# First pair of half-size products with plain work inside it, and a scan insert that ends with the state, in a Mamba-2 layer on one core

## The chip, the cores and the metric

The kernel runs on one core of a Trainium2 chip. Its time is the device time of one execution in microseconds (us). The core's engines run side by side: PE (TensorE) does the matmuls, ACT (ScalarE), DVE (VectorE) and POOL (GpSimd) the elementwise work, SP (SyncE) issues most of the transfers. Weights are loaded into PE on a path of its own (PEld in the profile).

## The reference

One layer of a hybrid trunk, cut to what is computed here (batch 1, 512 tokens, width 2048, 64 heads of 64 in 8 groups, state 128, all in float32):

```python
hn = rmsnorm(x, ln_g)
proj = hn @ w_in                      # z, (x, B, C), dt
xbc = silu(causal_depthwise_conv(xbc, conv_w, conv_b))
dt = softplus(dt + dt_bias); a = -exp(a_log)
# per chunk, for every head:
y_diag = einsum("blsg,blsgr,bsgrp->blgrp", cb, decay, xc)
y_off  = einsum("blgn,bgrpn,blgr->blgrp", cc, state, exp(cs))
new_state = state * exp(last) + einsum("bsgn,bsgr,bsgrp->bgrpn", bc, w_in, xc)
y = y_diag + y_off + d_skip * xs
y = rmsnorm(y * silu(z), norm_g)
out = rmsnorm(x + y @ w_out, final_g)
```

The in-projection has 80 column tiles of 128 (32 of z, 32 of x, 8 of B and 8 of C), the out-projection goes from 4096 to 2048.

## The kernel before

**Numbers in two parts.** Every float32 matmul is done in three, on a rounded part `hi` and a rest `lo`. `split_piece` (L84 to L89) makes both for a piece of weights: ACT casts `hi` (L87), DVE subtracts to get `lo` (L88). PE cannot use a piece before DVE is done with its `lo`.

**In-projection.** The first eight column tiles (B0, C0, x0, z0, x1, z1, B1, C1) are done plainly: `mm_k` (L198) runs 16 k-steps of six matmuls, 256 wide each. The other 72 tiles are done in 36 pairs by a scheme with seven half-size products instead of eight (`pair`, L639; each `product`, L635 to L637, has 24 matmuls of 256). The weights of the products are the quarters R11, R22, R21 and sums of quarters T1, T2, T3, T4: `q_fetch` adds a quarter in by an accumulating transfer of POOL, `q_add` (L604) adds on DVE. The product T4 of a pair is not run at once but handed to the next pair as `prev`, and runs there between the second and the third product: in a steady pair PE's order is R11, T1, the T4 of the pair before, T2, R22, R21, T3. The first pair has no such `prev`: its order is T1, R11, (nothing for four steps), R22, T2, R21, T3. R11 and T1 write the banks `S` and `R`, and so do T2 and R22 after them.

**Steps and events.** A step is the work of PE between two calls of `run`: one k-step of six matmuls of 256, or three of 512, about 0.68 us. A pair has 28. Whatever is to be done beside the matmuls is an event at a step (`add`, L704), and `run(step)` issues the events of a step just before its matmuls. PE, SP and POOL execute in the order of the code; on DVE and ACT a scheduler of the framework orders the instructions. `q_events` sets when the loads, sums and splits of a pair are issued, relative to the pair's first step `b`; `x_form3` (L571 to L578, steps 114 to 126) rewrites half of the activations `xh` and `xl` in place for the third product, over a temporary `xr` that the tiles' own normalization (L398) uses too.

**The scan.** Each of the 32 units (two heads) has six events: load, decay (12 exps on ACT, L456 to L459, and a product `m` on DVE, L461), transposes of x (L473, with `xd` and `xw` on DVE), state (four matmul records, L488, then split into `stsh` on ACT and `stsl` on DVE, L403 and L404), yd (16 records, L502 and L506, then DVE's D-skip, L509) and yo (L518 to L520, then DVE, L521 to L523). State and yd of a unit are due in the same step, b+9 of a pair; g_bt (L416) makes the transpose of B for a group and g_cb (L433 to L436) its products.

**Out-projection.** Plain pieces (`mm_o`, L929 to L931: 512 wide, six matmuls for each of four token tiles t) and two chains of four half-size pairs (`opair`, L867 to L869) alternate: 12 plain pieces, chain 1, eight plain pieces, chain 2, then plain pieces to the end. The chains use sums of quarters of y as well (`y_fetch` L822, `y_forms` L841 to L848, f11, f1, f2 and so on, each split into h and l). In a chain the first pair has no `prev` and the same order T1, R11, nothing, R22, T2 as above. L889 subtracts the T1 product from `acc`, L902 the R22 product and L907 the T2 product, L912 adds R21's; T3's is copied on ACT (L916). `get_out` loads and splits the plain pieces; every fourth goes to buffers of its own.

The list that follows shows the functions the diff touches and their callers.

## Time and profile before

| | us |
|---|---|
| median of 3 runs | 1294.51 (1292.67 to 1301.33) |
| profiled execution, its own time | 1295.7 |
| its span, first to last instruction | 1294.0 |
| mean granted clock of PE | 0.991 of full speed |
| PE, DVE, ACT busy | 1252.1, 1084.3, 826.6 |
| ACT's casts of whole pieces, all / DVE's splits of whole pieces, mean each | 1.05 / 1.22 |

The share of the span by engine in the profile's first part says which engine bounds the whole, the waits of PE say at which places another one does. Where a wait is named by a line, that line is where the awaited result was made.

### The profile page before, as it was taken

Reading aid. Unit: us, or ns where it says so; the run is one execution under the profiler, and the core shown is the slowest. Engines: PE = TensorE matmul, PEld = TensorE weight load, DVE = VectorE, ACT = ScalarE, POOL = GpSimd, SP = SyncE. Lnnn points to the kernel's source line nnn. Section 1 sums busy time; section 2 is a strip of 40 time slices with the busy share of each in tenths; the row PEclk is TensorE's granted clock in tenths of the full one; section 3 lists DMA queues with packets and bytes.
Section 4 is the critical chain, followed back from the end, with each engine's and each line's share of the span. In section 5 each row is a group of like instructions: output and inputs, shape, how many; then the busy total and the mean of one; then the engine's idle time right before and its main releaser. Section 6 shows DMA issues by size and latency. Waiting matters only on the chain.

```text
span 1294.0 us, 24519 instructions
## 1 busy us (share of the span) xinstructions
PE 1252.1 (97%) x9932; PEld 1192.9 (92%) x9932; DVE 1084.3 (84%) x1449; ACT 826.6 (64%) x1357; POOL 77.5 (6%) x99
## 2 busy tenths in 40 slices
PE   8989899999999999999999999999999899999997
PEld 8989899999999999999999999999988899899885
DVE  5796988988989898998889899889857877887865
ACT  7667667677666757767685867778666445434433
POOL 0000001010000101010100001000000000000000
PEclk9989999999999999999999999999999999999999
DMA  9546657585676667667667677766637576647612
GB/s 356 179 141 172 162 161 174 143 215 142 192 197 174 159 169 183 164 176 199 162 161 195 151 188 171 212 155 154 185 105 258 146 199 199 197 119 229 183 57 98
DMA packets 70194, 225.90 MB, mean 175 GB/s; under 512 B 8384, under 2 KB 12800, under 8 KB 69952
## 3 DMA queue, kind: packets, MB, share of 16 engines
q1 hardware_dynamic: 56688, 176.34, 40.2%
q0 software_dynamic: 12672, 46.14, 22.1%
q8 instruction: 78, 1.28, 0.4%
q10 hardware_dynamic: 720, 1.84, 0.4%
q14 instruction: 36, 0.29, 0.1%
HBM read 211.52 MB, written 12.78 MB: 173 GB/s over the span
## 4 chain that ended last, share of the span: by engine, by line
PE 74%; DVE 11%; DMA 7%; issue 4%; ACT 3%; SPq 0%; POOL 0%; DVEq 0%; ACTq 0%; POOLq 0%
PE S L637 7%; PE S L635 7%; PE S L636 7%; PE mm L635 5%; PE mm L636 4%; PE R L635 4%; PE mm L637 4%; PE R L636 4%; PE R L637 4%; DVE lo L88 3%; PE mm L929 3%; PE mm L931 3%; PE mm L930 3%; PE yd L502 2%; PE mm L867 2%
## 5 line engine op out<-in xcount | busy, mean ns | idle before, releaser
L87 ACT CAST hi<-ra 128x1024 fp32r<-128x1024 f32 x150 | 154.7, 1046 | 159.5 <-DVE ra L604 72.9
L88 DVE TENSOR_TENSOR lo<-ra,hi 128x1024 fp32r<-128x1024 f32 x150 | 181.3, 1221 | 24.2 <-ACT hi L87 24.1
L635 PE MATMUL mm<-xh,hi 128*128 128x256 f32 x576 | 163.6, 284 | 0.0
L637 PE MATMUL mm<-xh,lo 128*128 128x256 f32 x576 | 160.6, 279 | 0.6 <-DVE lo L88 0.6
L636 PE MATMUL mm<-xl,hi 128*128 128x256 f32 x576 | 160.4, 278 | 0.0
L637 PE MATMUL R<-s,lo 128*128 128x256 f32 x576 | 160.3, 278 | 0.1
L635 PE MATMUL R<-s,hi 128*128 128x256 f32 x576 | 160.2, 278 | 0.0
L636 PE MATMUL R<-s,hi 128*128 128x256 f32 x576 | 160.2, 278 | 0.0
L88 DVE TENSOR_TENSOR lo<-rc,hi 128x1024 fp32r<-128x1024 f32 x94 | 114.9, 1223 | 28.5 <-ACT hi L87 28.1
L87 ACT CAST hi<-rc 128x1024 fp32r<-128x1024 f32 x94 | 98.4, 1047 | 50.8 <-issue 29.1
L604 DVE TENSOR_TENSOR ra<-ra,rc 128x1024 f32<-128x1024 f32 x88 | 107.7, 1224 | 13.3 <-DMA rc<-in_wi 11.8
L635 PEld LDWEIGHTS mm<-xh,hi 128*128 128x128 f32 x576 | 108.1, 188 | 5.2 <-issue 5.0
L637 PEld LDWEIGHTS mm<-xh,lo 128*128 128x128 f32 x576 | 109.2, 190 | 0.8 <-DVE lo L88 0.8
L637 PEld LDWEIGHTS R<-s,lo 128*128 128x128 f32 x576 | 109.1, 189 | 0.3 <-DVE lo L88 0.3
L635 PEld LDWEIGHTS R<-s,hi 128*128 128x128 f32 x576 | 108.2, 188 | 0.0
L636 PEld LDWEIGHTS mm<-xl,hi 128*128 128x128 f32 x576 | 108.2, 188 | 0.0
L636 PEld LDWEIGHTS R<-s,hi 128*128 128x128 f32 x576 | 108.1, 188 | 0.0
L637 PE MATMUL S<-xh,lo 128*128 128x256 f32 x288 | 83.5, 290 | 5.6 <-DVE lo L88 5.6
L635 PE MATMUL S<-xh,h1h 128*128 128x256 f32 x288 | 83.4, 290 | 1.0 <-DVE xr L398 1.0
L635 PE MATMUL S<-xh,hi 128*128 128x256 f32 x288 | 81.3, 282 | 2.2 <-ACT xh L577 1.3
L636 PE MATMUL S<-xl,hi 128*128 128x256 f32 x288 | 81.2, 282 | 0.7 <-DVE xl L578 0.7
L636 PE MATMUL S<-xl,h1h 128*128 128x256 f32 x288 | 80.8, 280 | 0.0
(452 smaller groups left out, 3940.8 us busy)
## 6 DMA issues: line engine op xcount, KB each, us to landing
rc<-in_wi SPq DMA_DIRECT2D x76, 512.0 KB, 5.9
ra<-in_wi SPq DMA_DIRECT2D x42, 512.0 KB, 6.2
rb<-in_wi SPq DMA_DIRECT2D x40, 512.0 KB, 6.9
ra<-in_wi POOLq DMA_DIRECT2D x36, 512.0 KB, 6.3
rb<-in_wi POOLq DMA_DIRECT2D x36, 512.0 KB, 5.9
csb<-cscr SPq DMA_DIRECT2D x32, 512.0 KB, 8.0
ra<-in_wo SPq DMA_DIRECT2D x26, 512.0 KB, 5.4
yscr<-xs SPq DMA_DIRECT2D x32, 256.0 KB, 2.6
```

The source lines that it names most:

```text
L87: S.copy(out=hi, in_=raw)
L88: V.tensor_tensor(out=lo, in0=raw, in1=hi, op=ALU.subtract)
L502: T.matmul(pyd[r, i, :], x[:, 2 * i, hh, :], m[:, i, hh::4, :], start=i == 0, stop=False, skip_group_check=True)
L604: V.tensor_tensor(out=raw, in0=raw, in1=qs[n][other], op=ALU.add)
L635: T.matmul(ps, hi[:, k, :], ah, start=first and k == 0, stop=False, skip_group_check=True)
L636: T.matmul(ps, hi[:, k, :], al, start=False, stop=False, skip_group_check=True)
L637: T.matmul(ps, lo[:, k, :], ah, start=False, stop=k == KH - 1, skip_group_check=True)
L867: T.matmul(ps[:, t, :], yh[:, k, tt], hi[:, k, :], start=st, stop=False, skip_group_check=True)
L929: T.matmul(ps, yh, hi, start=first and k == 0, stop=False)
L930: T.matmul(ps, yh, lo, start=False, stop=False)
L931: T.matmul(ps, yl, hi, start=False, stop=last and k == 1)
```

## The change

Four edits. The first pair starts four steps earlier (`QB` is 124 instead of 128). The last four k-steps of the last plain tile, C1, which were run before the first pair, are handed to it as its `prev` and run at b+8, between T1 and T2, followed by `finish` of that tile. The first pair so gets the order of all the others, R11, T1, plain rest, T2, R22, R21, T3, and the special cases of its events (`lone`, `t1`) go.

The same is done at both chains of the out-projection: the last plain piece's token tiles 2 and 3 (12 matmuls of 512 wide) are handed to the first `opair` (`tail`, `bridge`), which gets the order R11, T1, rest, T2, R22; the base of the chain is four steps earlier; the y forms of the first chain are fetched and made at other offsets.

In `get_out` the pieces that use the separate buffers are those with n divisible by 4 (and not 0) instead of n%4 == 3.

In a step with several events of the scan, load, decay, transposes and yd are issued first, then g_bt and g_cb, and state and yo last; before, the g events came first, then for each unit load, decay, transposes, state, yd, yo.

```diff
+    QB = NPL * KT - 4
...
-            at[s] = NPL * KT + i * QS
+            at[s] = QB + i * QS
...
         late = 4 if i == 0 or type(blocks[i - 1]) is tuple else 0
+        late -= 4 if type(blocks[min(i + 1, len(blocks) - 1)]) is tuple else 0
...
-                                     *((op, ("oh", "ol")) if n % 4 == 3 else (wp,)))
+                                     *((op, ("oh", "ol")) if n and n % 4 == 0 else (wp,)))
...
-                        *(((5, q_split, ("R22",)), (9, q_split, ("T2",))) if lone else
-                          ((5, q_split, ("T2",)), (9, q_split, ("R22",)))),
+                        (5, q_split, ("T2",)), (9, q_split, ("R22",)),
...
-        if prev:
-            first(b)
-            second(b + 4)
-            prev(b + 8)
-        else:
-            second(b)
-            first(b + 4)
-            for i in range(8, 12):
-                run(b + i)
...
+        product(s_, W("R11"), 11, True, b)
...
+        product(r_, W("T1"), 1, True, b + 4)
...
+        prev(b + 8)
+        product(s_, W("T2"), 2, False, b + 12)
...
+        product(r_, W("R22"), 4, False, b + 16)
...
+    add_units((0, u_load), (1, u_decay), (2, u_xt))
+    add_units((4, u_yd))
     for g in range(1, G):
         add(at["B", g] + (30 if ("B", g) in plain else 93), g_bt, g)
...
-        w = ramp[u] if u < len(ramp) else [28, 42, 56, 65, 65, 71]
-        for o, f in zip(w, (u_load, u_decay, u_xt, u_state, u_yd, u_yo)):
-            add(at["x", u] + o, f, u)
+    add_units((3, u_state), (5, u_yo))
...
-        for k in range(KT):
+        for k in range(KT if n < NPL - 1 else KT - 4):
...
+    def prev(step):
+        for i in range(4):
+            run(step + i)
+            mm_k(ps, pieces[2 * NPL - 1], 4 + i, KT - 4 + i)
+        finish(NPL - 1, ps)
...
-                add(base[i] - ((50, 32), (54, 32))[m][j], y_fetch, m, j)
-                add(base[i] - ((39, 24), (47, 24))[m][j], y_forms, m, j)
+                add(base[i] - ((48, 30), (54, 32))[m][j], y_fetch, m, j)
+                add(base[i] - ((36, 23), (47, 24))[m][j], y_forms, m, j)
...
+        def tail(ps, w, y, t, s, first, step):
+            for k in range(2):
+                run(step + k)
+            mm_o(ps, w, y, t, first, True)
+            a = acc[:, t, s * L:(s + 1) * L]
+            with urgent():
+                V.tensor_tensor(out=a, in0=ps, in1=a, op=ALU.add)
...
+                    if type(blocks[kb + 1]) is tuple and s == 3 and n0 + 1 == n_end and t > 1:
+                        bridge.append(partial(tail, ps[t], opieces[n0], ys[p], t, s, p == pairs[0]))
+                        continue
```

How this moves instructions shows in the engines' orders. Lines of the changed kernel are numbered two or three higher in this part than those of the kernel before (L88 is L89, L604 is L607, L578 is L581). DVE in the first pair, before: `lo<-rc` is R22's rest, then `lo<-ra` T2's, `h1l` the R11 of pair 1, `ra<-ra,rc` the sum for T4, `lo<-rc` R21's, `lo<-rb` T3's; rows of `xr` and `xl` belong to `x_form3`.

```order
L88 TENSOR_TENSOR lo<-rc,hi 128x1024
L404 TENSOR_TENSOR stsl<-yo,stsh 128x128
L574 TENSOR_TENSOR xr<-xh 128x512
L88 TENSOR_TENSOR lo<-ra,hi 128x1024
L575 TENSOR_TENSOR xr<-xr,xl 128x512
L88 TENSOR_TENSOR h1l<-ra,h1h 128x1024
L576 TENSOR_TENSOR xr<-xr,xl 128x512
L604 TENSOR_TENSOR ra<-ra,rc 128x1024
L88 TENSOR_TENSOR lo<-rc,hi 128x1024
L578 TENSOR_TENSOR xl<-xr,xh 128x2x256
L88 TENSOR_TENSOR lo<-rb,hi 128x1024
```

And with the change, from the row of T4's sum to R21's rest, `m` being the scan's decay product (the rest of T2 stands two rows ahead of the first):

```order
L607 TENSOR_TENSOR ra<-ra,rc 128x1024
L581 TENSOR_TENSOR xl<-xr,xh 128x2x256
L407 TENSOR_TENSOR stsl<-yo,stsh 128x128
L577 TENSOR_TENSOR xr<-xh 128x512
L578 TENSOR_TENSOR xr<-xr,xl 128x512
L579 TENSOR_TENSOR xr<-xr,xl 128x512
L464 TENSOR_TENSOR m<-m,cbm 128x1536
L581 TENSOR_TENSOR xl<-xr,xh 128x2x256
L89 TENSOR_TENSOR h1l<-ra,h1h 128x1024
L577 TENSOR_TENSOR xr<-xh 128x512
L89 TENSOR_TENSOR lo<-rc,hi 128x1024
L578 TENSOR_TENSOR xr<-xr,xl 128x512
```

R22's rest was the first of the pair's rests there and is now behind the sum for T4, six rows of `x_form3`, `m` and the R11 of pair 1; T2's rest is now ahead of it.

PE at a scan insert in a steady pair, before (L488 is the state, L502 and L506 yd):

```order
L635 MATMUL mm<-xh,hi 128x256
L636 MATMUL mm<-xl,hi 128x256
L637 MATMUL mm<-xh,lo 128x256
L488 MATMUL yo<-xw,bt 128x128 x2
L502 MATMUL yd<-m,xd 64x256 x2
L506 MATMUL yd<-m,xd 64x128 x2
L502 MATMUL yd<-m,xd 64x256 x2
L506 MATMUL yd<-m,xd 64x128 x2
L635 MATMUL mm<-xh,hi 128x256
L636 MATMUL mm<-xl,hi 128x256
```

With the change (L491 is the state, L505 and L509 yd):

```order
L637 MATMUL mm<-xh,hi 128x256
L638 MATMUL mm<-xl,hi 128x256
L639 MATMUL mm<-xh,lo 128x256
L505 MATMUL yd<-m,xd 64x256 x2
L509 MATMUL yd<-m,xd 64x128 x2
L505 MATMUL yd<-m,xd 64x256 x2
L509 MATMUL yd<-m,xd 64x128 x2
L491 MATMUL yo<-xw,bt 128x128 x2
L637 MATMUL mm<-xh,hi 128x256
L638 MATMUL mm<-xl,hi 128x256
```

The state's matmuls were the first of the insert and are now the last.

DVE at the start of the first output chain, before (L604 sums T2, then `h1l` is the R11 of the next pair, `lo<-ra` T2's rest, `lo<-rc` R21's, `lo<-rb` T3's):

```order
L841 TENSOR_TENSOR f3l<-yr,f3h 128x512
L841 TENSOR_TENSOR f22l<-yr,f22h 128x512
L604 TENSOR_TENSOR ra<-ra,rc 128x1024
L952 SCALAR_TENSOR_TENSOR acc<-xt,rms,acc 128x512
L88 TENSOR_TENSOR h1l<-ra,h1h 128x1024
L88 TENSOR_TENSOR lo<-ra,hi 128x1024
L88 TENSOR_TENSOR lo<-rc,hi 128x1024
L88 TENSOR_TENSOR lo<-rb,hi 128x1024
L604 TENSOR_TENSOR ra<-ra,rc 128x1024
L902 TENSOR_TENSOR acc<-acc,mm 128x2x256
```

With the change (L993 adds the rest of the plain piece to `acc`, L882 subtracts T1's product, L886 T2's; `lo<-ra` is T2's rest, the two `lo<-rc` are R22's and R21's):

```order
L882 TENSOR_TENSOR acc<-acc,mm 128x2x256
L837 TENSOR_TENSOR f22l<-yr,f22h 128x512
L993 TENSOR_TENSOR acc<-mm,acc 128x512
L607 TENSOR_TENSOR ra<-ra,rc 128x1024
L993 TENSOR_TENSOR acc<-mm,acc 128x512
L930 SCALAR_TENSOR_TENSOR acc<-xt,rms,acc 128x512
L89 TENSOR_TENSOR lo<-ra,hi 128x1024
L89 TENSOR_TENSOR lo<-rc,hi 128x1024 x2
L607 TENSOR_TENSOR ra<-ra,rc 128x1024
L886 TENSOR_TENSOR acc<-acc,mm 128x2x256
L89 TENSOR_TENSOR lo<-rb,hi 128x1024
```

T2's rest stands behind the sums of the plain rest, and R22's, which stood far ahead of these rows, comes directly behind it.

## The prediction

> **What bounds the kernel now.** I read the first page, then the waits of PE stretch by stretch, then the windows for PE's clock, and last the rows of PE and DVE (TensorE and VectorE) at the places that the diff touches. The page's first part gives busy time, share of the span and instructions.

> ```profile
> PE 1252.1 (97%) x9932; PEld 1192.9 (92%) x9932; DVE 1084.3 (84%) x1449; ACT 826.6 (64%) x1357; POOL 77.5 (6%) x99
> ```

> PE is the bound: it idles 1294.0 − 1252.1 = 41.9 us in the whole span, part of that at the start, before the plain tiles. The change neither adds nor removes a matmul, so it can win only PE's stalls, the time lost to a low clock, and the pace of the matmuls. Where are the stalls that it can reach? The waits of PE (engine and line, what it waited for; us in total, times, longest) are, from 118 to 172 us, that is the last plain tile, pair 0 and half of pair 1:

> ```profile
> PE S L635 <- ACT xh L577: 1.3, 1, 1.3
> PE S L635 <- DVE xr L398: 1.0, 1, 1.0
> PE S L635 <- ACT hi L87: 0.9, 1, 0.9
> PE S L637 <- DVE lo L88: 0.8, 1, 0.8
> PE S L636 <- DVE xl L578: 0.7, 1, 0.7
> PE mm L637 <- DVE lo L88: 0.6, 1, 0.6
> ```

> They sum to 5.3 us. From 172 to 925 us, all the other pairs with the scan beside them, one row is left; behind it come the one row of the first plain output piece, the three rows of 990 to 1032 us (first output chain), the longer one of 1135 to 1200 us (second) and two of 1200 to 1225 us (the piece behind it):

> ```profile
> PE S L637 <- DVE lo L88: 4.8, 8, 1.5
> ...
> PE S L930 <- DVE lo L88: 0.5, 1, 0.5
> ...
> PE mm L867 <- DVE acc L907: 2.5, 1, 2.5
> PE mm L869 <- DVE lo L88: 1.4, 1, 1.4
> PE mm L867 <- ACT hi L87: 0.9, 1, 0.9
> ...
> PE mm L867 <- DVE acc L889: 1.7, 1, 1.7
> ...
> PE mm L867 <- ACT mm L916: 1.7, 1, 1.7
> PE mm L930 <- DVE lo L88: 1.2, 1, 1.2
> ```

> The windows show what follows some stalls (from:to, length, PE busy with its matmuls, granted clock, DMA share, GB/s):

> ```profile
> 163.00:166.00 3.00, 1.33 (x8) 0.95 0.30 122
> 145.20:148.60 3.40, 3.11 (x14) 0.51 0.39 77
> 165.70:169.10 3.40, 3.39 (x16) 0.50 0.66 193
> 498.00:502.00 4.00, 2.46 (x21) 1.00 0.50 186
> 1025.90:1029.30 3.40, 3.40 (x19) 0.50 0.37 83
> ```

> After the clustered stalls of pair 0, pair 1 and the first chain PE runs 3.4 us at half clock, which costs 1.7 us each time; 1.54 us of idle time at 498 us drew no such window. So the first pairs lose 5.3 + 2 × 1.7 = 8.7 us, the first chain 4.8 + 1.7 = 6.5 us.

> **The change, part by part.** First, the order of the first pair (with the 24 half-tile matmuls of C1's last four k-steps between T1 and T2). When does DVE deliver what PE wants? Its rows (start, duration, line, operation) give prices from start to start:

> ```profile
> 116.10 0.69 DVE L476 TENSOR_TENSOR xd<-tr,dt 128x512 f32<-128x512 f32 x1
> 116.70 0.68 DVE L574 TENSOR_TENSOR xr<-xh 128x512 f32<-128x512 f32 x1
> 117.30 0.42 DVE L479 TENSOR_TENSOR xw<-xd,win 128x256 f32<-128x256 f32 x1
> 117.63 0.69 DVE L575 TENSOR_TENSOR xr<-xr,xl 128x512 f32<-128x512 f32 x1
> 118.23 0.74 DVE L509 SCALAR_TENSOR_TENSOR xs<-xs,par,yd 128x512 f32<-128x512 f32 x1
> 118.89 0.69 DVE L576 TENSOR_TENSOR xr<-xr,xl 128x512 f32<-128x512 f32 x1
> 119.49 1.22 DVE L604 TENSOR_TENSOR ra<-ra,rc 128x1024 f32<-128x1024 f32 x1
> 120.63 0.69 DVE L578 TENSOR_TENSOR xl<-xr,xh 128x512 fp32r<-128x512 f32 x1
> ...
> 124.30 1.76 DVE L461 TENSOR_TENSOR m<-m,cbm 128x1536 f32<-128x1536 f32 x1
> 125.97 0.69 DVE L578 TENSOR_TENSOR xl<-xr,xh 128x512 fp32r<-128x512 f32 x1
> ```

> So a half-tile operation takes 0.60, a 256-wide one 0.33, a split or a sum of a whole piece 1.14, the scan's m 1.67. In the changed order DVE does, from xd (116.10) up to the end of R22's lo: 13 of the half-tile operations that rework xh and xl (7.8), five whole-piece operations (T2's sum and lo, T4's sum, h1l of pair 1's R11, R22's lo: 5.7), m (1.67), and xd, the D-skip of yd, the gate, three 256-wide ones and a 0.2 one (3.1): 18.2 us, which ends at 134.3. DVE ran back to back here before, so I take no gaps. PE's rows at the same place:

> ```profile
> 118.24 0.40 PE L198 MATMUL S<-xh,hi 128*128 128x256 f32 x2
> ...
> 124.12 0.61 PE L488 MATMUL yo<-xw,bt 128*128 128x128 f32 x4
> 124.69 0.28 PE L636 MATMUL S<-xl,h1h 128*128 128x256 f32 x1
> ```

> The row at 118.24 starts the step that is now the first pair's base. From it PE has four blocks of 24 (R11, T1, the plain rest, T2) of 2.8 us each, a state insert of 0.5 (124.12 to 124.69, less the matmul in it) and a transpose of about 0.5: it stands before R22 at 130.4. T2's lo comes at 124.9, in time; R22's, at 134.3, is 3.9 us late. That is one stall of 3.9 where there were six that sum to 5.3; behind it R21's lo (136.1), T3's (137.9), the reworked xh (138.8) and the z and S copies are all ahead of PE, which needs T3 at 140. A stall this long draws a half-clock window (1.7): 5.6 against 8.7, a gain of 3.1. Bounds: with no stall left +8.7; with DVE gaps of 2 us and a second window, −0.6.

> The plain rest keeps its weight buffer until about 127.4, and R22's split takes over that buffer; 1.05 of ACT and 1.14 of DVE behind 127.4 is 129.6, still ahead of 134.3, so this costs nothing unless DVE becomes early. The first pair's DMAs go out four steps (2.7 us) earlier with their events, on SP and POOL; no row of PE from 118 to 172 us names a DMA, so I count nothing.

> Second, the scan's inserts. Putting yd ahead of state frees the decay tile about 0.5 us earlier (124.12 to 124.69 is one state insert). ACT's next exps wait for that: the wait "ACT m L456 <- PE yd L506" has 24.5 us in 21 times between 170 and 930 us, and behind them in ACT's order stands the hi of T3, then DVE's lo for which PE waits 4.8 us in 8 places.

> ```profile
> ACT m L456 <- PE yd L506: 24.5, 21, 1.2
> ```

> Half a microsecond at each of eight is at most 4.0; most of them are shorter than that, and DVE's order behind ACT may swallow it. I take +1.5, between 0 and +3. The state now lands later relative to its reader yo, which stands six steps behind it: 6 × 0.68 = 4.1 us for a copy on ACT and one on DVE. The worst such copy before stood here:

> ```profile
> 913.40 0.61 PE L488 MATMUL yo<-xw,bt 128*128 128x128 f32 x4
> ...
> 917.25 0.28 DVE L404 TENSOR_TENSOR stsl<-yo,stsh 128x128 fp32r<-128x128 f32 x1
> ```

> It is done 4.1 us behind the state's start, and the others among these pairs within 2.2 us; the cover is thin once only, so I count nothing.

> The inserts also set the pace. Two stretches of undisturbed 256-wide matmuls:

> ```profile
> 252.20:280.80 28.60, 28.60 (x245) 1.00 0.75 216
> 1144.00:1178.00 34.00, 34.00 (x302) 1.00 0.69 186
> ```

> One runs at 116.7 ns each, the other at 112.6, at the same full clock. By the starts of PE's rows, 13 of the 28 state-and-yd inserts among the pairs leave the slower pace behind and 15 the faster, and it lasts some 113 matmuls: 113 × 4.1 ns = 0.46 us for each insert. Which pace follows when the state's matmuls are the last of the insert no row of before shows for a joined insert; the two state inserts that stand alone (at 103.5 and 124.1 us) kept the slower pace, the transposes alone left the faster one in 18 of 21. I take no change, between −15 × 0.46 = −7 and +13 × 0.46 = +6.

> Third, the output. Chain 1: DVE's rows and PE's wait before:

> ```profile
> 999.70 0.69 DVE L841 TENSOR_TENSOR f11l<-yr,f11h 128x512 fp32r<-128x512 f32 x1
> ...
> 1014.90 0.39 PE L867 MATMUL mm<-hi,f2h 128*128 128x256 f32 x1 [0.91 <-ACT hi L87]
> ```

> The y forms now go out two to three steps earlier, so f11l stands at 998 to 1000, and from it DVE's new order has 17.2 us of work until T2's lo is there (five whole-piece operations 5.7, one residual sum of 0.66 like the D-skip's, 18 half-tile ones 10.8): 1015.2 to 1017.2. PE is ready for T2 one product (2.8) earlier than its 1014.0 (1014.90 − 0.91) of before, at 1011.2: a stall of 4.0 to 6.0, with one half-clock window. 5.0 + 1.7 = 6.7 against 6.5, so −0.2, between −2.5 (a second window) and +2.5 (forms 2 us earlier still). The wait for acc (L907) goes, because T4's lo stands behind that subtraction in DVE's new order. In chain 2 the wait for acc L889 (R22 overwrites the bank from which that line still subtracts T1) goes, since the tail and T2 now lie between T1 and R22: +1.7 (0 to 1.7, if T2 is late in its turn). The piece behind it is split in the other pool: its wait for lo (1.2) may go, but the copy at L916 still waits behind forms; +0.5 (0 to 1.2). The first plain output piece loses its early place on DVE to the last pair's z and to xd, about two half-tile operations: −1.2 (−2 to 0). Two more table loads on ACT lie where ACT has slack: nothing.

> **The sum.** 3.1 + 1.5 + 0 − 0.2 + 1.7 + 0.5 − 1.2 = 5.4 us off the profiled execution, 1295.7 (its span 1294.0 and 1.7 around it), gives 1290.3. The median of the runs, 1294.51, is 1.2 below that execution, so the same gain there gives 1289.1; I say 1289.

> [...]

> **The rivals.** (a) The stalls simply close: DVE keeps up, and the 8.7 of the first pairs, 6.5 and 1.7 of the chains and 2.9 behind them go, 19.8 in all, with or without the scan's 4.8: 1270 to 1275. Against it stands DVE's count of 18.2 and 16.6 us: it is not moved earlier, only rearranged. (b) Slower: an insert that ends with the state leaves the slower pace behind. The two lone state inserts speak for it, the transposes of like shape against it. All 15 faster ones turned cost 15 × 0.46 = 7, and against the gain of 5.4 the time is 1296, slower by 1.5; it decides from 12 inserts on (12 × 0.46 = 5.5). (c) The stall only moves: the first pair and chain 1 each draw two half-clock windows (1.7 more each) and nothing comes from the scan: 5.4 − 3.4 − 1.5 = 0.5, so 1294. (d) The opposite of (b): all inserts leave the faster pace, 1289 − 6 = 1283.

> **How the numbers follow.** My forecast, 1285 to 1293, has 0.45; (a) 0.10; (b) 0.15; (c) 0.17; (d) 0.13. The range from 1281 to 1297 leaves out (a) and the tails of (b) and (d). One per cent, 12.9 us, is about what a measurement of this kernel can tell from no change. Faster than 1281.6 are (a) and a bit of (d): 0.12. Slower than 1307.5 needs (b) and (c) and more: 0.03. The rest, 0.85, is within 1%.

> **What would show it.** In the changed profile: one wait of PE for R22's lo of 3 to 5 us near 131 and none for xh, xl or xr between 136 and 146 (right), or none at all ((a)). The row for T3's lo between 172 and 925 us at 2 to 4 us instead of 4.8. In chain 1 a wait for T2's lo of 4 to 6 us in place of three waits, and none for acc; in chain 2 none for acc. The count of inserts that leave 113 ns or 117 ns behind decides (b) and (d). The prediction is wrong if DVE's order at run time has gaps that I left out, or if the pace shifts by more than ten inserts.

## The result: slower by about 1.1%

| | before | after |
|---|---|---|
| median, us | 1294.24 (1292.67 to 1301.33, 4 runs) | 1309.95 (1309.24 to 1310.21, 4 runs) |
| ratio to before | | 1.011, 95% interval 1.0072 to 1.0147 |
| span of the profiled execution, us | 1294.0 | 1308.2 |
| mean granted clock of PE | 0.991 | 0.985 |

The forecast was 1289, in a range from 1281 to 1297. Two lines of the changed kernel's page, the busy line and the one that says where the chain that ended last spent its time:

```profile
PE 1253.4 (96%) x9932; PEld 1189.9 (91%) x9932; DVE 1087.8 (83%) x1449; ACT 827.1 (63%) x1359; POOL 77.6 (6%) x99
...
DMA csb<-cscr 5%; DVE lo L89 5%; PE S L639 5%; PE S L637 4%; PE S L638 4%; PE mm L908 4%; PE mm L909 4%; PE mm L907 4%; PE mm L865 3%; PE mm L863 3%; PE mm L864 3%; PE R L638 2%; PE R L637 2%; PE R L639 2%; PE mm L637 2%
```

PE does the same work, but a transfer, the scan's load `csb<-cscr`, now stands first in that chain. Where did the time come from? The starts of PE's rows cut the span into stages (pairs counted from 0, each from the first matmul of its R11):

| stage, us | before | after | difference |
|---|---|---|---|
| start to pair 3 | 194.0 | 189.6 | −4.4 |
| pair 3 to pair 35 (scan beside the products) | 712.9 | 726.2 | +13.3 |
| pair 35 to the end (output) | 387.0 | 392.4 | +5.4 |
| span | 1294.0 | 1308.2 | +14.2 |

The waits of PE in the changed kernel, in the stretches that the prediction used: 118 to 172 us, 170 to 930, 990 to 1040, 1135 to 1240.

```profile
PE R L639 <- DVE lo L89: 2.9, 1, 2.9
PE S L639 <- DVE lo L89: 1.6, 1, 1.6
PE mm L639 <- DVE lo L89: 0.4, 1, 0.4
PE R L637 <- ACT hi L88: 0.3, 1, 0.3
...
PE S L639 <- DVE lo L89: 12.8, 15, 1.9
PE R L639 <- DVE lo L89: 2.4, 4, 0.8
PE R L637 <- ACT hi L88: 1.4, 2, 1.1
...
PE mm L907 <- ACT hi L88: 2.5, 1, 2.5
PE mm L863 <- ACT hi L88: 2.0, 1, 2.0
PE mm L865 <- DVE lo L89: 0.5, 1, 0.5
PE mm L908 <- DVE lo L89: 0.5, 1, 0.5
...
PE mm L863 <- ACT mm L894: 2.9, 1, 2.9
PE mm L865 <- DVE lo L89: 0.2, 1, 0.2
```

In the first pair one wait for R22's rest is left, as forecast; the 1.6 us behind it in the list are a wait for T3's rest in pair 1. Together the stalls of this stretch are 5.2 us, where they were 5.3. Of the 4.4 us up to pair 3, 1.6 had been won before the tile C1 began, where the change does nothing (its first matmul starts at 105.8 us, before at 107.4; PE ran 3.4 us at half clock near 80 us, before 6.8). In the output the clock was at half for 17.1 us, the end of the kernel left out, where it was 3.4; at half a us lost for each (256-wide matmuls start 0.213 us apart in the half-clock windows of the scan, mostly 0.113 at full clock), that is 6.8 us, more than the whole difference of 5.4.

In the scan the row for T3's rest has grown from 4.8 us in 8 places to 12.8 in 15, with 3.8 more at R22. The windows of the scan before and after, and of stretches behind four of the stalls (from:to, length, PE busy, clock, DMA share, GB/s):

```profile
194.00:907.00 713.00, 708.18 (x6142) 1.00 0.68 175
```

```profile
189.60:915.80 726.20, 709.49 (x6141) 0.99 0.66 172
...
132.60:136.00 3.40, 3.40 (x17) 0.52 0.90 141
501.30:504.70 3.40, 3.40 (x19) 0.51 0.96 319
...
1012.00:1022.00 10.00, 7.82 (x30) 0.66 0.62 191
1029.00:1037.00 8.00, 6.07 (x26) 0.59 0.54 165
```

PE is idle in the scan for 726.2 − 709.5 = 16.7 us where it was 4.8. The ends of matmuls are modelled and hide part of a stall, so the starts of the products' rows tell more. Sorted by the distance from one start to the next, the scan's difference of 13.3 is: longer gaps +16.7 (30.1 us where they were 13.3), half clock +4.1, inserts +0.5, and −8.0 from the pace: 4572 of the distances are near 113 ns and 562 near 118, where it was 2796 and 2422. So the change won 8 us by the pace and lost 21, nearly all of it in stalls and low clock.

**What makes T3's rest late?** DVE beside a scan insert in pair 12, before (the gate is L523, m is L461):

```profile
406.85 0.42 DVE L521 TENSOR_TENSOR ecs<-yo,ecs 128x256 f32<-128x256 f32 x1
...
407.84 0.42 DVE L522 TENSOR_TENSOR xs<-xs,ecs 128x256 f32<-128x256 f32 x1
...
408.84 0.69 DVE L523 TENSOR_TENSOR xs<-xs,z 128x512 f32<-128x512 f32 x1
409.44 1.75 DVE L461 TENSOR_TENSOR m<-m,cbm 128x1536 f32<-128x1536 f32 x1
```

and after (the gate is L526, m is L464):

```profile
405.86 0.42 DVE L525 TENSOR_TENSOR xs<-xs,ecs 128x256 f32<-128x256 f32 x1
...
406.86 1.75 DVE L464 TENSOR_TENSOR m<-m,cbm 128x1536 f32<-128x1536 f32 x1
408.53 0.69 DVE L526 TENSOR_TENSOR xs<-xs,z 128x512 f32<-128x512 f32 x1
```

Nobody asked for that in the change: with the events in another order the scheduler put m between the operations of yo, ahead of the gate, in 22 of the 32 units; before it was so in none. Counted from the start of its pair's R11, the gate ended at 16.4 us before and ends at 18.2 us now (medians of the 26 units between pair 3 and pair 35). What hangs on the gate is not PE but SP. SP issues the store of y (`yscr<-xs`, L524 before, L527 after) as soon as the gate is done (0.03 us behind its end in each of the 32 units, before and after), and the next weight loads and `csb` stand behind it in the same queue (the first load goes out 0.43 us after the store, median of both kernels). The waits of SP between 172 and 925 us, before and after:

```profile
SPq L524 <- DVE xs L523: 500.1, 28, 19.0
```

```profile
SPq L527 <- DVE xs L526: 508.8, 27, 20.8
```

For two thirds of the scan (500.1 and 508.8 of 753 us) SP does nothing but wait for the gate, and then issues the store and the loads one behind the other. SP's queue ahead of pair 11, before (the pair starts at 372.19 us) and after (369.19):

```profile
366.00 0.33 SPq L524 DMA_DIRECT2D yscr<-xs  x1
...
368.63 0.62 SPq L440 DMA_DIRECT2D csb<-cscr  x1
```

```profile
364.20 0.33 SPq L527 DMA_DIRECT2D yscr<-xs  x1
364.63 0.37 SPq L82 DMA_DIRECT2D rc<-in_wi  x1
...
366.06 0.38 SPq L82 DMA_DIRECT2D rb<-in_wi  x1
366.50 0.75 SPq L443 DMA_DIRECT2D csb<-cscr  x1
```

The store leaves 5.0 us ahead of the pair where it left 6.2 us ahead: 0.7 of that because the gate ends later in pair 10 (16.6 us for 15.9), 0.5 because pair 10 is shorter by the faster pace (21.6 us for 22.1). From there the 1.2 us go down to PE, in pair 11 of the changed kernel on ACT, DVE and PE:

```profile
375.54 0.40 ACT L459 ACTIVATE m<-csb,cs 128x128 f32<-128x128 f32 x1 [1.44 <-DMA csb<-cscr]
...
378.09 1.05 ACT L88 CAST hi<-rc 128x1024 fp32r<-128x1024 f32 x1
...
379.18 1.22 DVE L89 TENSOR_TENSOR lo<-rc,hi 128x1024 fp32r<-128x1024 f32 x1 [3.47 <-ACT hi L88]
...
386.75 1.22 DVE L89 TENSOR_TENSOR lo<-rb,hi 128x1024 fp32r<-128x1024 f32 x1
...
388.03 0.38 PE L639 MATMUL S<-xh,lo 128*128 128x256 f32 x1 [1.65 <-DVE lo L89]
```

ACT waits 1.44 us for `csb` ahead of the casts (0.39 before), so R22's hi is late, DVE idles 3.47 us for it (2.37 before), everything behind it on DVE slips, T3's rest too, and PE stops 1.65 us (0.47 before).

One thing in this chain is less simple than it looks: m did not pass the gate of pair 10. In pairs 5, 10, 15, 20, 25 and 30 the gate kept its place and still ends 0.7 to 2.5 us later in its pair than before, and the stalls of over 1 us stand in the pairs right behind these (T3's in 6, 11, 16, 21 and 31, R22's in 26). In the kernel before the larger stalls stood in 11, 16, 21 and 26 as well. The loads of pair 10 hang on the gate of pair 9, which m did pass, so the delay would be handed on from pair to pair; this was not followed step by step. Whether the place of the gate is the cause is therefore left to the experiments.

### The profile page after: what moved, and what is told of

Read it like the earlier page. It is cut to its first block, busy times and chain, and to the rows that moved or that the text cites. A ratio compares the mean times of both kernels' runs of the same rounds, so it can differ in the third digit from the quotient of the medians.

```text
span 1308.2 us, 24517 instructions
## 1 busy us (share of the span) xinstructions
PE 1253.4 (96%) x9932; PEld 1189.9 (91%) x9932; DVE 1087.8 (83%) x1449; ACT 827.1 (63%) x1359; POOL 77.6 (6%) x99
## 3 DMA queue, kind: packets, MB, share of 16 engines
q10 hardware_dynamic: 720, 1.84, 0.4%
## 4 chain that ended last, share of the span: by engine, by line
PE 58%; DVE 19%; DMA 10%; ACT 7%; issue 5%; SPq 1%; DVEq 0%; ACTq 0%
DMA csb<-cscr 5%; DVE lo L89 5%; PE S L639 5%; PE S L637 4%; PE S L638 4%; PE mm L908 4%; PE mm L909 4%; PE mm L907 4%; PE mm L865 3%; PE mm L863 3%; PE mm L864 3%; PE R L638 2%; PE R L637 2%; PE R L639 2%; PE mm L637 2%
## 5 line engine op out<-in xcount | busy, mean ns | idle before, releaser
L88 ACT CAST hi<-ra 128x1024 fp32r<-128x1024 f32 x153 | 158.4, 1047 | 170.5 <-DVE ra L607 108.4
L89 DVE TENSOR_TENSOR lo<-ra,hi 128x1024 fp32r<-128x1024 f32 x153 | 186.6, 1221 | 18.1 <-ACT hi L88 16.7
L637 PE MATMUL R<-s,hi 128*128 128x256 f32 x576 | 161.2, 280 | 1.7 <-ACT hi L88 1.7
L637 PE MATMUL mm<-xh,hi 128*128 128x256 f32 x576 | 161.9, 281 | 0.0
L89 DVE TENSOR_TENSOR lo<-rc,hi 128x1024 fp32r<-128x1024 f32 x92 | 112.3, 1222 | 32.1 <-ACT hi L88 31.8
L607 DVE TENSOR_TENSOR ra<-ra,rc 128x1024 f32<-128x1024 f32 x88 | 107.7, 1224 | 27.4 <-DMA rc<-in_wi 25.6
L88 ACT CAST hi<-rc 128x1024 fp32r<-128x1024 f32 x92 | 96.0, 1046 | 40.7 <-issue 20.6
L637 PEld LDWEIGHTS R<-s,hi 128*128 128x128 f32 x576 | 109.7, 191 | 2.3 <-ACT hi L88 2.3
L638 PEld LDWEIGHTS R<-s,hi 128*128 128x128 f32 x576 | 109.7, 190 | 0.0
L637 PEld LDWEIGHTS mm<-xh,hi 128*128 128x128 f32 x576 | 108.3, 188 | 0.1
L637 PE MATMUL S<-xh,h1h 128*128 128x256 f32 x288 | 82.5, 287 | 0.0
L637 PE MATMUL S<-xh,hi 128*128 128x256 f32 x288 | 81.1, 282 | 0.0
```

The source lines that it names most:

```text
L88: S.copy(out=hi, in_=raw)
L89: V.tensor_tensor(out=lo, in0=raw, in1=hi, op=ALU.subtract)
L607: V.tensor_tensor(out=raw, in0=raw, in1=qs[n][other], op=ALU.add)
L637: T.matmul(ps, hi[:, k, :], ah, start=first and k == 0, stop=False, skip_group_check=True)
L638: T.matmul(ps, hi[:, k, :], al, start=False, stop=False, skip_group_check=True)
```

## The experiments

Two theories stood against each other for the scan: **A**, the new insert order moved m ahead of the gate, and the gate holds the loads in SP's queue; **B**, the pairs that start four steps earlier shift the scan against the loads. **C** and **D** were that the insert itself, or DVE's order itself, makes the splits late. For the output, **F** was that a load stands behind a fetch of y, **G** that the choice of buffers costs. Medians are beside runs of the kernel before on the same chip (1294.79, 1293.19 and 1294.79 us for e1 to e4, e5 to e8, e9 to e12); ratios are to those.

| run | what it is | median, us | ratio (95%) | to pair 3 / scan / output, us |
|---|---|---|---|---|
| e1 | after, old insert order | 1297.23 | 1.0019 (1.0000 to 1.0037) | 191.7 / 714.2 / 389.1 |
| e2 | before, new insert order | 1306.65 | 1.0089 (1.0056 to 1.0122) | 189.8 / 725.8 / 391.7 |
| e3 | after, gate ahead of m | 1292.09 | 0.9984 (0.9961 to 1.0006) | 191.7 / 711.2 / 385.9 |
| e4 | after, store of y later | 1275.11 | 0.9846 (0.9819 to 0.9873) | 190.9 / 702.3 / 378.6 |
| e5 | before, first pair alone | 1293.44 | 1.0000 (0.9984 to 1.0016) | 191.5 / 713.3 / 384.6 |
| e6 | before, output part alone | 1297.95 | 1.0040 (1.0019 to 1.0062) | 193.3 / 714.7 / 388.6 |
| e7 | before, store of y later | 1281.45 | 0.9919 (0.9894 to 0.9944) | 190.7 / 708.6 / 383.3 |
| e8 | first pair, new inserts, store later | 1274.43 | 0.9860 (0.9836 to 0.9883) | 190.2 / 702.1 / 379.8 |
| e9 | e6, fetch of y later | 1292.07 | 0.9983 (0.9962 to 1.0005) | 192.6 / 716.2 / 383.3 |
| e10 | e6, old buffers | 1295.91 | 1.0015 (0.9997 to 1.0033) | 194.4 / 717.5 / 386.5 |
| e11 | e4, fetch of y later | 1275.12 | 0.9850 (0.9821 to 0.9880) | 189.7 / 703.9 / 378.4 |
| e12 | e11, gate ahead of m | 1274.96 | 0.9846 (0.9814 to 0.9878) | 189.1 / 702.4 / 379.1 |

### Is it the insert order? (e1, e2)

e1 puts the six calls back in their old order in the changed kernel, e2 puts the new order into the kernel before:

```diff
-    add_units((0, u_load), (1, u_decay), (2, u_xt))
-    add_units((4, u_yd))
...
-    add_units((3, u_state), (5, u_yo))
+        for o, f in zip(w, (u_load, u_decay, u_xt, u_state, u_yd, u_yo)):
+            add(at["x", u] + o, f, u)
```

> The changed kernel with the old order of the scan's events (state ahead of yd). DVE's order then has the gate of y ahead of the decay product m again. Theory A (the new insert order made the scheduler put m ahead of the gate; the store of y leaves SP 1.7 us later and the weight loads queue behind it): the scan from pair 3 to pair 35 returns from 726.2 us to about 713, and the median from 1310 to 1296 or 1297. Theory B (the pairs that start four steps earlier shift the scan against the loads): the scan stays at about 726 and the median near 1310.

> The kernel before with only the order of the scan's events changed. Theory A: the scan from pair 3 to pair 35 goes from 712.9 us to about 726 and the median from 1294 to 1307 or 1308. Theory B: nothing of the loss appears, 1294 or less.

The scan took 714.2 us in e1 and 725.8 in e2, as theory A had it; B falls. T3's row between 170 and 930 us, in e1 and in e2:

```profile
PE S L639 <- DVE lo L89: 3.6, 8, 1.6
```

```profile
PE S L637 <- DVE lo L88: 14.0, 15, 1.8
```

The new order alone costs 12 us of the median. Its profiled execution is also 4.7 us longer in the output (391.7 against 387.0), which e2 leaves as it was; two more half-clock windows there (6.8 us, half of it lost) make 3.4 of that. Such differences of a single execution say little: e5, with the same output too, has none of these windows before the end and is 2.4 us shorter there than the kernel before. The pace goes with the insert too: 2277 distances near 113 ns and 2940 near 118 in e1, 4232 and 934 in e2.

### Is it the gate, and by which path? (e3, e4)

e3 raises the priority of yo's three operations on DVE, so that in those 22 units the gate stands ahead of m again; the state stays last in the insert:

```diff
+        with urgent():
             V.tensor_tensor(out=ecs, in0=pyo, in1=ecs, op=ALU.mult)
             V.tensor_tensor(out=y[:, 2 * P:L], in0=y[:, 2 * P:L], in1=ecs, op=ALU.add)
             V.tensor_tensor(out=y, in0=y, in1=z, op=ALU.mult)
```

e4 leaves DVE's order and issues the store later, which puts it behind the next four weight loads of SP's queue:

```diff
+    def u_store(u):
+        nc.sync.dma_start(yscr[u // UPG][:, u % UPG, :], un[u]["y"])
...
-        nc.sync.dma_start(yscr[u // UPG][:, u % UPG, :], y)
...
+    for u in range(NU):
+        add(at["x", u] + steps[u][5] + 8, u_store, u)
```

> The changed kernel with yo's three operations of DVE at high priority, so that the gate of y stands ahead of m on DVE while the state stays last in the insert. Theory A: the stalls in the scan fall from 30 us to about 13 and its half-clock windows go, while the faster pace of the matmuls stays (8 us), so the scan takes about 705 us and the median is near 1289. Theory C (the insert with the state last is itself what makes T3's weights late): the scan stays at about 726 us, 1310.

> The changed kernel with m still ahead of the gate on DVE, but the store of y issued eight steps later, behind the next four weight loads in SP's queue. Theory A with the queue as its path: the loads no longer wait for the gate, the stalls go, the scan takes 705 us or less, median 1289 or less. Theory D (DVE's order itself makes the splits late, by the 1.7 us of m ahead of them): the scan stays at about 726 us, 1310.

PE's waits from 170 to 930 us in e3:

```profile
PE S L640 <- DVE lo L89: 7.7, 13, 1.8
```

and in e4, with SP's first wait between 172 and 925 us:

```profile
PE S L641 <- DVE lo L89: 1.1, 6, 0.2
PE mm L639 <- ACT mm L670: 0.7, 1, 0.7
```

```profile
SPq L82 <- DVE lo L89: 565.0, 90, 12.8
```

e3 puts back only the place of the gate and takes 15 us off the scan, 711.2 against 726.2, with R22's waits gone and one half-clock window in place of three: the place of the gate is the greater part of the loss, and C, by which the scan would have stayed at 726, falls. But e3 came out between the two expectations, not at 705. Its gate ends 16.25 us into the pair, a little earlier than before the change, and still 7.7 us of T3 waits are left, more than the 4.8 of before. The faster pace brings PE to T3 sooner, while a split on DVE took 1.22 us and a cast on ACT 1.05 before and after the change; that would explain it, but no run tested it alone.

e4 decides for the queue: m still stands ahead of the gate, the gate still ends 18.1 us into its pair, and yet T3's waits fall to 1.1 us; SP now waits for the splits that free its buffers (565 us in that row) and hardly for the gate. D falls, and the scan at 702.3 is shorter than e3's.

### How much is each other part worth? (e5, e6, e7, e8)

e5 and e6 take one part of the change each, e7 moves the store in the kernel before, e8 leaves the output as it was beside the rest of e4.

> The kernel before with the first pair's new start and order alone; scan inserts and output as before. My theory: the first pairs win 3 to 4 us up to pair 3 (194.0 to about 190.5), scan and output stay at 713 and 387 us, median 1290 to 1291.5. Rival (the four steps also move the scan or the output): the gain is gone or doubled by the end.

> The kernel before with the change at the output chains and the choice of buffers alone. From e1, in which pair 35 to the end took 389.1 against 387.0 us: the output loses 1 to 4 us, mostly in a wait of the last plain piece ahead of chain 1 for ACT's hi, median 1295 to 1298. Rival (the output part gains by itself and lost only by late loads from the scan): median 1290 to 1293.

> The kernel before with the store of y issued eight steps later, nothing else. Theory A: the gate held up the loads before the change too, only less; the 4.8 us of T3 stalls in the scan mostly go and the output gains some: median 1285 to 1290. Rival E (the gate was early enough before; e4 won by the new insert with it): 1293 to 1295.

> First pair and scan inserts as changed, store of y eight steps later, output and its buffers as before the change. If the output part is worth nothing or costs, this is at 1275 or below; if it wins what the forecast gave it (2 us in chain 2, nothing in chain 1) with the loads out of the way, 1276 to 1279.

e5's profiled execution is 2.5 us shorter up to pair 3, but its median, 1293.44 against 1293.19, misses the expected 1290 to 1291.5: it shows no gain, and the interval leaves room for one of 2 us at most. The single profiles differ in part by how many half-clock windows fell there: from C1's first matmul to pair 3 the eight with the new first pair take 83.2 to 83.8 us and the six with the old one 82.0 to 86.6, with two such windows in the kernel before and none in e2, the 82.0. e6 costs 4.8 us by the medians, somewhat more than the 1 to 4 that were expected of the output; the interval is about 2.5 to 8 us. e7 shows that the gate held up the loads before the change too: with the store later T3's waits of 4.8 us are down to this,

```profile
PE S L639 <- DVE lo L88: 0.9, 5, 0.3
```

and the median falls by 0.8%, further than to the 1285 that was expected at best; rival E falls. e8 is as fast as e4, so once loads arrive in time the output part shows no worth either way that could be measured.

### What does the output lose alone? (e9, e10, e11, e12)

e9 moves one number of e6, and e10 puts the old choice of buffers back:

```diff
-                add(base[i] - ((48, 30), (54, 32))[m][j], y_fetch, m, j)
+                add(base[i] - ((48, 28), (54, 32))[m][j], y_fetch, m, j)
```

> As e6 (output part alone), with the second fetch of y for chain 1 two steps later, so that the load of the last plain piece stands ahead of it in SP's queue, as it did before the change. Theory F (in e6 that load waits behind the fetch, which waits for its buffers until 993.8 us, and the 2.4 us wait for ACT's hi and a half-clock window come from it): the wait goes, the output from pair 35 to the end falls from 388.6 to 383 to 386 us, median 1292 to 1295. Rival (the cast itself is late on ACT, behind the scaling of y): the wait stays, 1298.

> As e6 with the old choice of buffers in get_out (n%4 == 3). If the new choice costs (theory G: the last plain piece of a block lost its own buffer and is split late), the wait for ACT's hi ahead of chain 1 goes and the median is at 1294 or 1295. If Theory F holds alone, that wait stays, and a wait for the split of the first piece behind a chain may come on top: 1298 to 1300.

> e4 (the changed kernel with the store of y eight steps later) with the fetch of y two steps later as in e9. In e4 no wait for ACT's hi is left ahead of chain 1, so by theory F nothing is to be won: 1274 to 1276, as e4.

> e11 with the gate of y also ahead of m on DVE. If the gate mattered only through SP's queue, nothing more is won with the store out of the queue's way: 1273 to 1276. If DVE's order costs by itself, 1270 or below.

In e6 SP issues the fetch of y and, behind it, the last plain piece; ACT scales the fetched y ahead of that piece's cast; PE waits:

```profile
993.84 1.49 SPq L821 DMA_DIRECT2D yr<-yscr  x2
995.38 0.42 SPq L82 DMA_DIRECT2D ra<-in_wo  x1
...
998.29 1.34 ACT L824 ACTIVATE yr<-yr,par 128x512 f32<-128x512 f32 x2 [9.53 <-DMA yr<-yscr]
...
1002.64 2.00 ACT L88 CAST hi<-ra 128x1024 fp32r<-128x1024 f32 x2 [0.26 <-DMA ra<-in_wo]
```

```profile
PE mm L913 <- ACT hi L88: 2.4, 1, 2.4
```

In e9 the piece is loaded ahead of the fetch, and from 985 to 1030 us only two waits are left, both at T2's place of chain 1:

```profile
PE mm L869 <- ACT hi L88: 1.8, 1, 1.8
PE mm L871 <- DVE lo L89: 0.8, 1, 0.8
```

The output took 383.3 us against 388.6, and the ratio to the kernel before fell from 1.0040 to 0.9983, with intervals that do not overlap: F holds. In e10, whose profiled execution is the slowest of its ten, a wait of 4.7 us for the cast into the old buffer stood at the same place, so the new choice of buffers is not what makes the wait, and G falls. The median of 1295.91 lies between the two expectations and within e6's reach, so e10 shows the wait and not the price of the buffers. e11 and e12 gain nothing over e4: with the store out of the way neither the fetch nor the place of the gate matters. Since e12 differs from e11 by the place of the gate alone, this also says that the swap on DVE costs through SP's queue and not by itself. e4, e8, e11 and e12 beat both kernels by 1.4% to 1.5% (against before) and agree among each other within a microsecond.

## Why the prediction was wrong, point by point

**First pair (+3.1 forecast).** Right for pair 0: one wait for R22's rest, 2.9 us where 3.9 was forecast, a half-clock window behind it (0.52 from 132.6 to 136.0), the waits for xh, xl and xr gone. Wrong for pair 1: the forecast took all the stalls up to 172 us as replaced by that one, but T3's weights in pair 1 are still late (1.6 us, before 0.9 and 0.8), so the stalls sum to 5.2 and not to 3.9. What the profile gained there is mainly one half-clock window of two (3.4 us, half of it lost), and e5's median shows no gain.

**The scan's inserts (+1.5 forecast, between 0 and +3).** This is the step that failed. It looked at two consequences of PE's new order, the decay tile that yd ahead of the state frees for ACT's exps, and the state's reader yo. It said of the stall at T3 that it would be shorter, 2 to 4 us in all; it was 12.8. It did not follow what the scheduler did with DVE's order in the steady pairs, where m passed the gate in 22 of 32 units, nor what is queued behind the store that waits for the gate. The gate's end moved by 1.8 us (about the price of m, 1.67, which the prediction had), and T3's wait more than doubled. The loss is 21 us in the scan before the pace. That the insert order brings it is shown by e1 and e2, that most of it hangs on the place of the gate by e3, and that it goes through SP's queue by e4 and e12.

**The pace (0, between −7 and +6).** Rival (d) came true: the joined insert that ends with the state leaves the faster pace. It is worth 8.0 us by the count of distances, more than the +6 that the prediction allowed: that counted 13 inserts with 113 matmuls each, 1469 at the slower pace, where the scan before had 2422. It hid part of the loss; that the total came out no worse than 1.1% is owed to it in part, and was not foreseen.

**Chain 1 (−0.2) and the last plain piece.** The stall for T2's weights came as one of hi (2.0) and lo (0.5), 2.5 us where 4 to 6 were forecast. The wait for acc went, as forecast. But the wait of 2.5 us for ACT's hi of the last plain piece ahead of the chain, with its long low-clock stretch (0.66 from 1012 to 1022 us), was not forecast: the fetch of y went out two steps earlier and so ahead of that piece's load in SP's queue (e6, e9). Again a queue, again SP. The first plain output piece lost 1.5 us (waits of 1.2 and 0.8 where there was one of 0.5), near the −1.2 that was forecast.

**Chain 2 (+1.7) and what follows.** The wait for acc L889 went, and the one for lo behind the chain too. PE's wait for T3's copy (L894, before L916) was 2.9 us where it was 1.7. From its first matmul to its last the chain took 89.7 us where it took 85.8; about 2.7 of that is the plain work that moved in (12 matmuls), and it has a half-clock window that the chain before did not have (3.4 us).

**Rivals and chances.** (a) was wrong; (b) had the sign of the pace wrong; (c) had more half-clock windows and no gain from the scan, but ended at 1294. Slower by over 1% had 0.03. None of the rivals had a queue of loads behind a late store, though the waits of SP, 500 us for that one row, stood in the profile before.

## What to carry to other kernels

In this kernel a store that waited for compute, in a queue that also issued loads, made the compute in front of it a gate for the loads behind it: read what the issuing queue waits for and which loads stand behind it, and put the store behind the loads (here 1281 against 1293 us in the kernel before, 1275 against 1310 in the changed one). The length of the queue's wait is no measure by itself: in e4 SP waits even longer, for buffers, and nothing is late. When a change alters the order in which code issues its work, read the new order on every engine and queue whose rows the changed pieces touch, even on engines that the edit does not name; here one swap on DVE, which nobody wrote, outweighed all that was gained.

## What the runs showed of the hardware

Two paces of the same 256-wide matmuls at the same granted clock, about 113 and 118 ns from start to start, go with the insert: where it ended with the state's four records, the faster one followed far more often (562 against 2422 slow distances in the scan). With the new order the slow distances were also few in e2 (934), e3 (736) and e4 (704), with the old one many in e1 (2940) and e7 (2493). Of the 20 inserts of state and yd alone between pair 3 and pair 35, 11 left mostly the slower pace behind before and 13 in e1, none with the change and one in e2. What in the insert does it was not looked into.

The half clock does not follow the length of the last stall alone: a stall of 1.84 us at 498 us was followed by 3.4 us at half clock (0.51 from 501.3 us), one of 1.83 us at 614 us by a full clock:

```profile
500.07 0.38 PE L639 MATMUL S<-xh,lo 128*128 128x256 f32 x1 [1.84 <-DVE lo L89]
...
615.58 0.38 PE L639 MATMUL S<-xh,lo 128*128 128x256 f32 x1 [1.83 <-DVE lo L89]
```

```profile
616.00:620.00 4.00, 4.00 (x37) 1.00 0.80 269
```
